# The RWKV recurrence gives each copying engine PSUM tiles of its own

## The chip, the cores and the metric

The kernel runs on one core of a Trainium2 chip. The time is that of one execution on the device, in microseconds: the median over the timed runs. A profiled execution also gives a trace with the start and length of every instruction on the core's engines: TensorE (PE, and PEld for its weight loads), VectorE (DVE), ScalarE (ACT), GpSimd (POOL) and SyncE (SP, which here issues most DMAs). The trace also gives the TensorE clock that was granted, where 1.00 is 2.4 GHz and 0.50 is 1.2 GHz.

## The reference

The reference runs a two-layer block (a sparse-attention mixer and an RWKV-7 mixer, each with a squared-ReLU MLP) and then a second block (two SwiGLU layers around a convolution and mLSTM mixer) over 512 tokens of width 1024. The change touches only the recurrence of the RWKV mixer, which for 16 heads of 64 channels keeps a 64x64 state and updates it token by token:

```
def step(state, inp):
    r_t, w_t, k_t, v_t, kk_t, b_t = inp
    sa = jnp.einsum('bhvk,bhk->bhv', state, -kk_t)
    state = (state * w_t[:, :, None, :] + sa[..., None] * b_t[:, :, None, :]
             + v_t[..., None] * k_t[:, :, None, :])
    y = jnp.einsum('bhvk,bhk->bhv', state, r_t)
    return state, y
```

The outputs y are then normalised per head, scaled, given a bonus term, multiplied by a gate and sent through an output matrix.

## The kernel before

The whole model is one program. Its instructions stand on each engine in the order in which the code writes them; each engine works off its own queue in that order, and semaphores hold an instruction until what it needs is done. The framework gives tiles out of pools in rotation: a new tile of a pool takes the buffer of an old one, and its first writer waits until the old one's readers are done.

The 512 tokens of the recurrence are cut into eight chunks of 64 (0 to 7). Within a chunk the token-by-token recurrence is written as matrix products, for 8 head pairs m and the two heads g of a pair; a head's half of the 128 partitions is LO (g = 0) or HI (g = 1). The function `recurrence` does for chunk c, in this order:

- R: right sides, `kl` times `sv` (L1920), 8 matmuls of K = 128 for m = 0 to 3 and 8 for m = 4 to 7, into one PSUM tile. ScalarE copies each half to `Rs` (L1922).
- TT: a triangular inverse times `Rs` (L1927), in two halves as well, into one PSUM tile. Of each half ScalarE copies the LO partitions and VectorE the HI partitions to `uv` (L1929, L1930).
- KR: `kr` times `sv`, 16 matmuls for the next state (L1935) and 16 for the outputs (L1938).
- BN: `bn` times `uv`, added to the next state (L1942); ScalarE copies its LO half and VectorE its HI half to `SV[c + 1]` (L1943, L1944). The next chunk's R needs both.
- MT: `mt` times `uv`, added to the outputs (L1949); ScalarE copies both halves to `Yn` (L1951).

Between these parts `beside(1)` puts work that does not depend on the state. A local group is one step of `local(c + 1)`: 8 matmuls of `KR` and `BK` (L1781) into a tile of two banks (`pG`, index g chooses the bank), a ScalarE copy to BN (L1782), and VectorE's mask products to MT (L1783) and KL (two, L1787). There are four local groups a chunk, and the last two quarters of the next chunk's KL come from the third and fourth. The other work is a step of `outputs`: for every second chunk it squares the outputs and takes their statistics (L1820 to L1826, `Yn` of two chunks at once; they run in chunks 2, 4 and 6), and later transposes them, multiplies by the gate and splits them into high and low parts (L1796 to L1808); its last part stands right after chunks 3 and 5, ahead of the next R. In chunk 7 there are no local groups, and output-matrix products (`part`) take the place of BN.

The PSUM tiles of R, TT, KR with BN, KR with MT, and the transposes come from pool `psC` (4 banks, one tile each). The local groups have `psG` (2 tiles of two banks).

For each chunk SyncE loads KL, SV and UV (two DMAs of 128 KB each), TT (256 KB), KR and BK (512 KB each) from DRAM, in an order that the code sets; a load waits in that queue until its buffer's last readers are done.

Of the kernel before, what the change touches and what calls it, by code (L numbers as in the profile page):

```python
# [178 lines left out]
class Kernel:  # L179
# [1556 lines left out]
    def recurrence(self, d, EC, sources, gate, nxt):  # L1736
# [3 lines left out]
        nc, tc = self.nc, self.tc  # L1740
        ident = self.c("ident")
        LO, HI = slice(0, 64), slice(64, 128)
# [145 lines left out]
        for c in range(8):  # L1888
# [15 lines left out]
            def group():  # L1904
                return psC.tile([128, 8, 64], F32, name="mm")
# [7 lines left out]

                return ((m, g, HALF[g]) for m in ms for g in G)

            parts = [range(4 * h, 4 * h + 4) for h in range(2)]
            p = group()
            for ms in parts:
                for m, g, s in each(ms):
                    nc.tensor.matmul(p[s, m], kl[:, g, m], sv[:, g, m], start=True, stop=True)  # L1920
                at = slice(ms[0], ms[-1] + 1)
                nc.scalar.copy(Rs[:, at], p[:, at])  # L1922
            beside(1)
            p = group()
            for ms in parts:
                for m, g, s in each(ms):
                    nc.tensor.matmul(p[s, m], TT[c][s, m], Rs[s, m], start=True, stop=True)  # L1927
                at = slice(ms[0], ms[-1] + 1)
                nc.scalar.copy(uv[LO, 0, at], p[LO, at])  # L1929
                nc.vector.tensor_copy(uv[HI, 1, at], p[HI, at])  # L1930
            beside(1)
            if c < 7:
                p = group()
                for m, g, s in each():
                    nc.tensor.matmul(p[s, m], kr[s, 2, m], sv[s, g, m], start=m == 0, stop=False)  # L1935
            py = group()
            for m, g, s in each():
                nc.tensor.matmul(py[s, m], kr[s, 1, m], sv[s, g, m], start=m == 0, stop=False)  # L1938
            beside(1)
            if c < 7:  # L1940
                for m, g, s in each():
                    nc.tensor.matmul(p[s, m], bn[:, g, m], uv[:, g, m], start=False, stop=m == 7)  # L1942
                nc.scalar.copy(SV[c + 1][LO, 0], p[LO])  # L1943
                nc.vector.tensor_copy(SV[c + 1][HI, 1], p[HI])  # L1944
            else:
                part(0, 0)
            beside(1)
            for m, g, s in each():
                nc.tensor.matmul(py[s, m], mt[:, g, m], uv[:, g, m], start=False, stop=m == 7)  # L1949
            for g, s in enumerate(HALF):  # L1950
                nc.scalar.copy(yn[:, g], py[s])  # L1951
            if c % 2 == 1:
                for g in outs:
                    step(g, 100)
# [307 lines left out]
```

## Time and profile before

| what | value |
|---|---|
| median of 3 timed runs | 2447.26 us (2445.79 to 2448.89) |
| the profiled execution's own time | 2448.56 us |
| its span, first to last instruction | 2446.8 us |
| PE busy over the span | 2296.2 us (94%), 12820 matmul records |
| DVE, ACT, POOL busy | 1396.6 us (57%), 1012.5 us (41%), 427.1 us (17%) |
| mean granted TensorE clock | 0.968 |

The span is 1.8 us shorter than the profiled execution's time. Busy shares are means over stages with different limits; the recurrence takes from about 935 to 1042 us of the span. In a timeline, rows of one line that follow each other closely are merged (x16 is 16 records; an fp32 matmul leaves two records), and the bracket gives the engine's idle time before the row and what ended it.

### The profile page before, as it was taken

Reading aid. Unit: us, or ns where it says so; the run is one execution under the profiler, and the core shown is the slowest. Engines: PE = TensorE matmul, PEld = TensorE weight load, DVE = VectorE, ACT = ScalarE, POOL = GpSimd, SP = SyncE. Lnnn points to the kernel's source line nnn. Section 1 sums busy time; section 2 is a strip of 40 time slices with the busy share of each in tenths; the row PEclk is TensorE's granted clock in tenths of the full one; section 3 lists DMA queues with packets and bytes.
Section 4 is the critical chain, followed back from the end, with each engine's and each line's share of the span. In section 5 each row is a group of like instructions: output and inputs, shape, how many; then the busy total and the mean of one; then the engine's idle time right before and its main releaser. Section 6 shows DMA issues by size and latency. Waiting matters only on the chain. (4 is left out here: it accounts for less than half of the span.)

```text
span 2446.8 us, 33701 instructions
## 1 busy us (share of the span) xinstructions
PE 2296.2 (94%) x12820; PEld 1886.1 (77%) x12820; DVE 1396.6 (57%) x2525; ACT 1012.5 (41%) x1903; POOL 427.1 (17%) x430
## 2 busy tenths in 40 slices
PE   7979999999988797789999999999989998999997
PEld 5768888888766676678888888888878886888886
DVE  7987544435788854664444456354466765534445
ACT  5567423324565364443323343332345544333232
POOL 4664100000454731220000020000021013000002
PEclk9999999999989898999999999999999999999998
DMA  4420333233324346432223223223223221323222
GB/s 145 113 75 9 104 98 100 90 99 105 104 69 136 120 142 205 139 104 95 95 95 101 91 84 104 96 94 104 86 76 96 85 79 61 104 95 101 98 89 67
DMA packets 98162, 241.80 MB, mean 99 GB/s; under 512 B 18121, under 2 KB 36937, under 8 KB 98001
## 3 DMA queue, kind: packets, MB, share of 16 engines
q1 hardware_dynamic: 95808, 234.46, 30.4%
q0 software_dynamic: 1040, 3.51, 0.4%
q8 instruction: 101, 1.65, 0.3%
q10 hardware_dynamic: 1152, 1.68, 0.2%
q14 instruction: 61, 0.49, 0.1%
HBM read 214.62 MB, written 19.22 MB: 96 GB/s over the span
## 5 line engine op out<-in xcount | busy, mean ns | idle before, releaser
L147 DVE TENSOR_TENSOR wlo<-wraw,whi 128x512 fp32r<-128x512 f32 (+2 forms) x702 | 513.1, 751 | 447.5 <-ACT whi L146 446.9
L358 PE MATMUL mm<-xh,whi 128*128 128x512 f32 (+3 forms) x1720 | 692.9, 403 | 19.8 <-ACT whi L146 8.2
L359 PE MATMUL mm<-xl,whi 128*128 128x512 f32 (+3 forms) x1720 | 684.1, 398 | 10.0 <-DVE xl L268 8.8
L360 PE MATMUL mm<-xh,wlo 128*128 128x512 f32 (+3 forms) x1720 | 682.8, 397 | 8.7 <-DVE wlo L147 8.6
L146 ACT CAST whi<-wraw 128x512 fp32r<-128x512 f32 (+2 forms) x721 | 430.0, 612 | 522.7 <-PE mm L359 474.4
L358 PEld LDWEIGHTS mm<-xh,whi 128*128 128x128 f32 (+3 forms) x1720 | 329.8, 192 | 96.9 <-issue 12.7
L360 PEld LDWEIGHTS mm<-xh,wlo 128*128 128x128 f32 (+3 forms) x1720 | 329.2, 191 | 83.9 <-DVE wlo L147 12.2
L359 PEld LDWEIGHTS mm<-xl,whi 128*128 128x128 f32 (+3 forms) x1720 | 329.9, 192 | 82.5 <-DVE xl L268 13.2
L358 PE MATMUL mm<-uh,whi 128*128 128x512 f32 (+1 forms) x900 | 346.7, 385 | 0.0
L360 PE MATMUL mm<-uh,wlo 128*128 128x512 f32 (+1 forms) x900 | 344.7, 383 | 0.0
L359 PE MATMUL mm<-ul,whi 128*128 128x512 f32 (+1 forms) x900 | 341.6, 380 | 0.0
L284 POOL TENSOR_TENSOR acc<-acc,sq 128x512 f32<-128x512 f32 (+1 forms) x55 | 73.2, 1331 | 1446.7 <-ACT sq L283 1446.3
L360 PEld LDWEIGHTS mm<-uh,wlo 128*128 128x128 f32 x900 | 168.9, 188 | 36.4
L359 PEld LDWEIGHTS mm<-ul,whi 128*128 128x128 f32 x900 | 169.0, 188 | 34.9
L358 PEld LDWEIGHTS mm<-uh,whi 128*128 128x128 f32 x900 | 169.2, 188 | 31.1
L423 ACT ACTIVATE u<-t 128x512 f32<-128x512 f32 x64 | 40.5, 632 | 192.7 <-DVE t L422 192.7
L422 DVE SCALAR_TENSOR_TENSOR t<-mm,rs 128x512 f32<-128x512 f32 x64 | 44.2, 691 | 89.6 <-PE mm L360 89.3
L436 DVE TENSOR_TENSOR x<-mm,x 128x512 f32<-128x512 f32 x64 | 44.2, 691 | 87.3 <-PE mm L360 87.3
L425 DVE TENSOR_TENSOR ul<-u,uh 128x512 fp32r<-128x512 f32 x64 | 44.3, 692 | 81.1 <-ACT uh L424 81.1
L267 ACT ACTIVATE xh<-x,vec 128x512 fp32r<-128x512 f32 (+1 forms) x50 | 35.2, 705 | 86.0 <-DVE x L436 22.0
L584 ACT CAST uh<-a 128x512 fp32r<-128x512 f32 x44 | 27.3, 621 | 76.4 <-DVE a L583 76.4
L268 DVE SCALAR_TENSOR_TENSOR xl<-x,vec,xh 128x512 fp32r<-128x512 f32 (+1 forms) x50 | 45.2, 908 | 23.5 <-ACT xh L267 23.3
(513 smaller groups left out, 2920.7 us busy)
## 6 DMA issues: line engine op xcount, KB each, us to landing
wraw<-in_ffn_in SPq DMA_DIRECT2D x88, 512.0 KB, 3.7
wraw<-in_up SPq DMA_DIRECT2D x64, 512.0 KB, 3.7
wraw<-in_down SPq DMA_DIRECT2D x64, 512.0 KB, 3.7
wraw<-in_rwkv SPq DMA_DIRECT2D x34, 512.0 KB, 4.8
wraw<-in_ffn_out SPq DMA_DIRECT2D x32, 512.0 KB, 3.7
wraw<-in_mix SPq DMA_DIRECT2D x32, 512.0 KB, 3.7
wraw<-in_dsa SPq DMA_DIRECT2D x23, 512.0 KB, 4.3
wraw<-in_ffn_out SPq DMA_DIRECT2D x16, 384.0 KB, 3.1
```

The source lines that it names most:

```text
L146: self.nc.scalar.copy(hi[:, :per], t)
L147: self.low.tensor_sub(lo[:, :per], t, hi[:, :per].bitcast(F32))
L267: nc.scalar.activation(hi, x, AF.Copy, scale=gm)
L268: nc.vector.scalar_tensor_tensor(lo, x, gm, hi.bitcast(F32), op0=OP.mult, op1=OP.subtract)
L284: (low or (nc.vector if m == NB - 1 else nc.gpsimd)).tensor_add(acc, acc, q[:, s])
L358: nc.tensor.matmul(ps, w[0], x[0], start=start, stop=False)
L359: nc.tensor.matmul(ps, w[0], x[1], start=False, stop=False)
L360: nc.tensor.matmul(ps, w[1], x[0], start=False, stop=stop)
L422: nc.vector.scalar_tensor_tensor(t, p, 0.0, self.rs, op0=OP.max, op1=OP.mult)
L423: nc.scalar.activation(u, t, AF.Square)
L425: nc.vector.tensor_sub(lo, u, hi.bitcast(F32))
L436: nc.vector.tensor_add(self.x[m], p, self.x[m])
```

## The change

The right sides of m = 0 to 3 and of m = 4 to 7 now lie in two PSUM tiles; ScalarE copies the first to `Rs`, VectorE the second. TT runs in one go for all m, with the LO results in one tile and the HI results in another; each engine copies its 64 partitions in one instruction. The next state's sums lie in two tiles in the same way. The KR matmuls for the next state stand right behind TT, ahead of the second local group; those for the outputs stand behind the third local group, after BN. A chunk takes seven tiles from `psC` instead of four.

```diff
--- before.py
+++ after.py
@@ -1913,42 +1913,39 @@
 
                 return ((m, g, HALF[g]) for m in ms for g in G)
 
-            parts = [range(4 * h, 4 * h + 4) for h in range(2)]
-            p = group()
-            for ms in parts:
-                for m, g, s in each(ms):
+
+            for h, copy in enumerate((nc.scalar.copy, nc.vector.tensor_copy)):
+                p, at = group(), slice(4 * h, 4 * h + 4)
+                for m, g, s in each(range(4 * h, 4 * h + 4)):
                     nc.tensor.matmul(p[s, m], kl[:, g, m], sv[:, g, m], start=True, stop=True)
-                at = slice(ms[0], ms[-1] + 1)
-                nc.scalar.copy(Rs[:, at], p[:, at])
+                copy(Rs[:, at], p[:, at])
             beside(1)
-            p = group()
-            for ms in parts:
-                for m, g, s in each(ms):
-                    nc.tensor.matmul(p[s, m], TT[c][s, m], Rs[s, m], start=True, stop=True)
-                at = slice(ms[0], ms[-1] + 1)
-                nc.scalar.copy(uv[LO, 0, at], p[LO, at])
-                nc.vector.tensor_copy(uv[HI, 1, at], p[HI, at])
-            beside(1)
+            ps2 = [group() for _ in G]
+            for m, g, s in each():
+                nc.tensor.matmul(ps2[g][s, m], TT[c][s, m], Rs[s, m], start=True, stop=True)
+            nc.scalar.copy(uv[LO, 0], ps2[0][LO])
+            nc.vector.tensor_copy(uv[HI, 1], ps2[1][HI])
             if c < 7:
-                p = group()
+                ps2 = [group() for _ in G]
                 for m, g, s in each():
-                    nc.tensor.matmul(p[s, m], kr[s, 2, m], sv[s, g, m], start=m == 0, stop=False)
-            py = group()
-            for m, g, s in each():
-                nc.tensor.matmul(py[s, m], kr[s, 1, m], sv[s, g, m], start=m == 0, stop=False)
+                    nc.tensor.matmul(ps2[g][s, m], kr[s, 2, m], sv[s, g, m], start=m == 0, stop=False)
             beside(1)
             if c < 7:
                 for m, g, s in each():
-                    nc.tensor.matmul(p[s, m], bn[:, g, m], uv[:, g, m], start=False, stop=m == 7)
-                nc.scalar.copy(SV[c + 1][LO, 0], p[LO])
-                nc.vector.tensor_copy(SV[c + 1][HI, 1], p[HI])
+                    nc.tensor.matmul(ps2[g][s, m], bn[:, g, m], uv[:, g, m], start=False, stop=m == 7)
+                nc.scalar.copy(SV[c + 1][LO, 0], ps2[0][LO])
+                nc.vector.tensor_copy(SV[c + 1][HI, 1], ps2[1][HI])
             else:
                 part(0, 0)
             beside(1)
+            p = group()
             for m, g, s in each():
-                nc.tensor.matmul(py[s, m], mt[:, g, m], uv[:, g, m], start=False, stop=m == 7)
+                nc.tensor.matmul(p[s, m], kr[s, 1, m], sv[s, g, m], start=m == 0, stop=False)
+            beside(1)
+            for m, g, s in each():
+                nc.tensor.matmul(p[s, m], mt[:, g, m], uv[:, g, m], start=False, stop=m == 7)
             for g, s in enumerate(HALF):
-                nc.scalar.copy(yn[:, g], py[s])
+                nc.scalar.copy(yn[:, g], p[s])
             if c % 2 == 1:
                 for g in outs:
                     step(g, 100)
```

In VectorE's queue, chunk 1 before: masks of the first local group, the two UV copies, masks of the second and third, the SV copy, masks of the fourth. In brackets stand the engines (and DMA queues) whose signals an instruction waits for.

```order
L1783 TENSOR_TENSOR MT<-pG,con 128x2x128 [waits DVE_49,Activation_49]
L1787 TENSOR_TENSOR KL<-pG,con 64x128 [waits DMAHW1_49,DMAHW0_49,DVE_49]
L1787 TENSOR_TENSOR KL<-pG,con 64x128
L1930 COPY UV<-mm 64x256 [waits Activation_49] x2
L1783 TENSOR_TENSOR MT<-pG,con 128x2x128 [waits Activation_49]
L1787 TENSOR_TENSOR KL<-pG,con 64x128 x2
L1783 TENSOR_TENSOR MT<-pG,con 128x2x128 [waits Activation_49]
L1787 TENSOR_TENSOR KL<-pG,con 64x128 x2
L1944 COPY SV<-mm 64x512 [waits DMAHW3_49,DMAHW2_49,Activation_49]
L1783 TENSOR_TENSOR MT<-pG,con 128x2x128 [waits Activation_49]
```

After, in the same chunk, from its new Rs copy on:

```order
L1921 COPY Rs<-mm 128x256 [waits DVE_49,PE_49]
L1783 TENSOR_TENSOR MT<-pG,con 128x2x128 [waits Activation_49]
L1787 TENSOR_TENSOR KL<-pG,con 64x128 [waits DMAHW1_49,DMAHW0_49]
L1787 TENSOR_TENSOR KL<-pG,con 64x128
L1927 COPY UV<-mm 64x512 [waits PE_49]
L1783 TENSOR_TENSOR MT<-pG,con 128x2x128 [waits Activation_49]
L1787 TENSOR_TENSOR KL<-pG,con 64x128 x2
L1937 COPY SV<-mm 64x512 [waits DMAHW2_49,DMAHW3_49,PE_49,Pool_49]
L1783 TENSOR_TENSOR MT<-pG,con 128x2x128 [waits Activation_49]
```

VectorE has one Rs copy more and one UV copy fewer, its SV copy stands ahead of the third group's masks, and its copies of UV and SV wait for PE where they waited for Activation (ScalarE).

On TensorE, chunk 1, the difference (- before, + after; the eight matmuls of each local group, L1781, are left out but for the first and last of a place):

```order
 L1781 MATMUL pG<-KR_7434,BK_7435 64x192
-L1927 MATMUL mm<-Rs,TT_8214 64x64 x16
+L1925 MATMUL mm<-Rs,TT_8214 64x64 x16
+L1931 MATMUL mm<-SV,KR_7433 64x64 x16
...
-L1935 MATMUL mm<-SV,KR_7433 64x64 x16
-L1938 MATMUL mm<-SV,KR_7433 64x64 x16
+L1935 MATMUL mm<-UV,BN 64x64 x16
...
-L1942 MATMUL mm<-UV,BN 64x64 x16
+L1943 MATMUL mm<-SV,KR_7433 64x64 x16
...
-L1949 MATMUL mm<-UV,MT 64x64 x16
+L1946 MATMUL mm<-UV,MT 64x64 x16
```

The state's KR matmuls moved from behind the second local group to ahead of it, next to TT; the outputs' KR matmuls moved from ahead of the third local group to behind it, past BN.

In VectorE's queue, chunk 2, behind the statistics of the norm (the last of them is L1191), before:

```order
L1191 SCALAR_TENSOR_TENSOR y_8792<-t_8793,y_8792 128x16 [waits DVE_49]
L1783 TENSOR_TENSOR MT<-pG,con 128x2x128 [waits Activation_49]
L1787 TENSOR_TENSOR KL<-pG,con 64x128 x2
L1826 TENSOR_TENSOR z<-Yn,y_8792 128x2x8x64 [waits DVE_49]
L1944 COPY SV<-mm 64x512 [waits DMAHW5_49,DMAHW4_49,Activation_49]
L1783 TENSOR_TENSOR MT<-pG,con 128x2x128 [waits Activation_49]
L1787 TENSOR_TENSOR KL<-pG,con 64x128 x2
```

After, up to the next chunk's Rs copy:

```order
L1191 SCALAR_TENSOR_TENSOR y_8812<-t_8813,y_8812 128x16 [waits DVE_49]
L1937 COPY SV<-mm 64x512 [waits DMAHW5_49,DMAHW4_49,PE_49]
L1783 TENSOR_TENSOR MT<-pG,con 128x2x128 [waits Activation_49]
L1787 TENSOR_TENSOR KL<-pG,con 64x128 x2
L1826 TENSOR_TENSOR z<-Yn,y_8812 128x2x8x64 [waits DVE_49]
L1783 TENSOR_TENSOR MT<-pG,con 128x2x128 [waits Activation_49]
L1787 TENSOR_TENSOR KL<-pG,con 64x128 x2
L1921 COPY Rs<-mm 128x256 [waits PE_49]
```

The SV copy moved ahead of the third group's masks and of the product z (L1826); the masks of the third and fourth group stay behind the statistics, and the next chunk's Rs copy follows them.

## Rows read from the trace of the kernel before

**Rows 1.** The stage's window: busy us (instructions) per engine, PEclk, DMA share, GB/s.

```profile
935.46:1041.77 106.31, 80.04 (x1966) 70.89 (x1966) 59.13 (x171) 43.26 (x111) 19.23 (x11) 0.92 0.53 163
```

**Rows 2.** Waits in the stage: who waited for whom, us in total, times, longest.

```profile
PE mm L1927 <- DVE UV L1930: 13.0, 8, 1.8
...
PE mm L1920 <- ACT Rs L1922: 9.3, 8, 1.9
...
PE mm L1920 <- DVE SV L1944: 3.1, 3, 1.5
```

**Rows 3.** Timeline of PE, chunk 1: start, us, instruction, idle before and its releaser.

```profile
950.07 0.64 PE L1920 MATMUL mm<-SV,KL 128*64 128x64 f32 x16
951.91 0.69 PE L1920 MATMUL mm<-SV,KL 128*64 128x64 f32 x16 [1.20 <-ACT Rs L1922]
...
955.41 0.62 PE L1927 MATMUL mm<-Rs,TT 64*64 64x64 f32 x13 [1.76 <-DVE UV L1930]
...
956.37 1.09 PE L1935 MATMUL mm<-SV,KR 64*64 64x64 f32 x31
957.29 1.03 PE L1938 MATMUL mm<-SV,KR 64*64 64x64 f32 x29
...
958.92 1.15 PE L1942 MATMUL mm<-UV,BN 128*64 128x64 f32 x32
960.00 0.88 PE L1781 MATMUL pG<-KR,BK 64*64 64x128 f32 x16
960.81 1.15 PE L1949 MATMUL mm<-UV,MT 128*64 128x64 f32 x32
961.79 0.64 PE L1920 MATMUL mm<-SV,KL 128*64 128x64 f32 x16
```

**Rows 4.** The same view, VectorE and ScalarE, chunk 1: masks, UV, SV.

```profile
954.30 0.59 DVE L1787 TENSOR_TENSOR KL<-pG,con 64x128 f32<-64x128 f32 x2
954.92 0.43 DVE L1930 COPY UV<-mm 64x256 f32<-64x256 f32 x1
...
960.16 0.58 ACT L1943 COPY SV<-mm 64x512 f32<-64x512 f32 x1 [0.74 <-PE mm L1942]
960.77 0.69 DVE L1944 COPY SV<-mm 64x512 f32<-64x512 f32 x1 [0.29 <-ACT SV L1943]
```

**Rows 5.** The same view: square and reduce of chunk 2, last masks.

```profile
968.73 1.06 ACT L1820 ACTIVATE z<-Yn 128x1024 f32<-128x1024 f32 x1
...
969.82 1.22 DVE L1822 TENSOR_REDUCE v<-z 128x16 f32<-128x1024 f32 x1
...
975.67 0.61 DVE L1787 TENSOR_TENSOR KL<-pG,con 64x128 f32<-64x128 f32 x2
```

**Rows 6.** The same view: start of chunk 4, last low parts (xl).

```profile
989.19 0.69 PE L1920 MATMUL mm<-SV,KL 128*64 128x64 f32 x16
...
990.74 0.88 DVE L1808 TENSOR_TENSOR xl<-ot,xh 128x128 fp32r<-128x128 f32 x4
```

**Rows 7.** The same view: chunk 0 and the issue of BK.

```profile
936.70 1.89 DVE L147 TENSOR_TENSOR wlo<-wraw,whi 128x512 fp32r<-128x512 f32 x3 [1.44 <-ACT whi L146]
...
938.03 0.69 PE L1920 MATMUL mm<-SV,KL 128*64 128x64 f32 x16 [1.89 <-ACT Rs L1922]
...
942.78 0.32 SPq L1206 DMA_DIRECT2D BK<-BKD  x1
```

**Rows 8.** DMA issues from 937 to 943 us: tile, KB, median us to landing.

```profile
BK<-BKD SPq DMA_DIRECT2D x1, 512.0 KB, 8.2
```

**Rows 9.** All six BK transfers of the stage.

```profile
DMA to landing us min/median/max: 5.5/5.9/8.2
```

**Rows 10.** Windows in which the clock fell, columns as in rows 1.

```profile
940.00:946.00 6.00, 4.44 (x84) 4.35 (x84) 2.86 (x8) 1.18 (x4) 0.57 (x1) 0.50 1.04 269
980.00:984.00 4.00, 4.00 (x84) 4.00 (x86) 1.43 (x4) 0.74 (x2) 0.86 (x2) 0.57 0.72 212
1032.00:1038.00 6.00, 5.07 (x68) 4.77 (x65) 1.45 (x5) 0.99 (x4) 1.81 (x1) 0.50 0.51 163
```

## Prediction

> **What bounds the kernel now.** I read the table of busy times first, then the stage that the diff touches, then its waits, then one turn of its loop. Over the whole span TensorE is the busiest engine by far; in the recurrence, from the first right-side matmul (935.46 us) to the end of the last output matmul (1041.77), it is busy 80.04 of 106.31 us [rows 1]. So this stage of eight chunks holds 26.3 us in which TensorE idles, and nothing else of the program moves: the order on SyncE and GpSimd stays as it is, and what follows the stage starts from its last output copies and shifts with them.
>
> The waits name the idle time [rows 2]: 13.0 us (8 times) are TT matmuls (L1927) behind VectorE's UV copy, 9.3 us (8 times) the second half of the right sides (L1920) behind ScalarE's Rs copy, 3.1 us (3 times) the first half behind VectorE's SV copy: 25.4 together. A chunk shows how [rows 3]. The first half's matmuls fill a PSUM tile, the second half wants the same tile and has to wait 1.20 us until ScalarE has copied the first, which it does only after two Yn copies; the second half of TT waits 1.76 us until VectorE has copied the first half of UV. VectorE comes late for two reasons [rows 4]: the mask products of a local group (L1783, L1787) stand ahead of it until 954.89, and out of a tile that both copy it starts only when ScalarE is done, as SV shows: ScalarE from 960.16 for 0.58, VectorE at 960.77.
>
> A second loss is the clock: 6.00 us at 0.50 (1.2 GHz) with 4.44 us busy in chunk 0, 4.00 us at 0.57 fully busy in chunk 3, 6.00 us at 0.50 with 5.07 busy in chunk 7 [rows 10]. Busy time times what the clock lacks is 2.2 + 1.7 + 2.5 = 6.4 us. Work at full clock is thus 80.04 − 6.4 = 73.6 us.
>
> **The change part by part.** *Ordinary chunk.* Chunk 1 lasts 961.79 − 950.07 = 11.72 us, without its two waits 8.76 [rows 3]. The prices in it: KR 957.29 − 956.37 = 0.92; a TT half, which is half as many matmuls of that shape, 0.46; a TT half with a local group 956.37 − 955.41 = 0.96, so the group 0.5; a group after KR 958.92 − 957.29 − 0.92 = 0.71; one after BN 0.81.
>
> The right sides now fill two tiles, so the 1.20 us wait goes: R (1.23 us), a local group (0.5), then TT at 1.73. ScalarE's half of Rs is ready 951.91 − 950.07 = 1.84 us after R's start, as the old second half shows. VectorE's half costs what its UV copy of as many elements a partition costs, 0.43 [rows 4], right behind R's end: ready at 1.85. So TT waits 0.1. The two half copies of UV become one of 64x512 on each engine, 0.58 and 0.69 as SV has them. VectorE's masks ended 954.89 − 952.60 = 2.3 us after R's end (951.91 + 0.69); its UV copy would end at 3.0. TensorE meanwhile does group and TT, 0.96 + 0.46, KR 0.92 and a group 0.71: 3.0 us. So BN finds UV just ready, with nothing to spare. This is the cover that shrank, as the 16 output KR matmuls (L1938) moved from ahead of BN to behind it: whatever VectorE is later, BN waits. SV's copies run side by side under a group, KR, a group and MT, over 3 us. I put 0.1 us in each of seven chunks: 0.7.
>
> *Chunk 0.* TT's first half waits for ScalarE until 938.03 [rows 7], where TensorE now is ready at 937.2: 0.8. Its second half waits for VectorE's Rs copy, queued behind three wlo products until 936.70 + 1.89 = 938.59, plus 0.43: until 939.07 instead of 938.49, 0.6.
>
> *Chunk 1, a new wait.* Chunk 0 ends at 935.46 + 8.76 + 1.4 = 945.6, and its successor's first local group would start at 946.9. It needs BK, issued at 942.78 and 8.2 us under way: 951.0 [rows 7, 8]. The issue hangs on SyncE's earlier queue, which this change leaves in its order, so I leave the time. Wait: 4.1 us. The six BK transfers took 5.5 to 8.2 us [rows 9]; with 5.5 the wait is 1.4. I take 8.2, since it is this transfer's own row.
>
> *Chunks 3, 5, 7.* In chunks 2, 4, 6 VectorE works off the norm statistics. From the reduce at 969.82 to the end of the last mask at 975.67 + 0.61 it needs 6.46 us [rows 5]; the same instructions stand there after, only the SV copy is moved ahead. The reduce can start when the second local group is copied by ScalarE (some 0.5 with its start) and the square is done (1.06): 1.84 + 0.92 + 0.92 + 0.71 + 0.5 + 1.06 = 6.0 us into the chunk; the last mask ends at 12.5. The next chunk's last quarter of R needs it and would start at 8.86 + 0.92 = 9.8. So each of the three odd chunks waits 2.7 us: 8.1. Before, chunks like these waited for SV and Rs.
>
> *Chunks 4 and 6.* At their start VectorE still has the transposed outputs: its last low part ends at 990.74 + 0.88 = 991.62, 2.43 us after R's start at 989.19 [rows 6]. The Rs copy stands behind it and ends at 2.9; TT's second half could start at 2.3: 0.6 each, 1.2.
>
> *Chunk 7* has no local group under its Rs copies: 0.15 us.
>
> New waits: 0.7 + 1.4 + 4.1 + 8.1 + 1.2 + 0.15 = 15.7 us instead of 26.3. At full clock the stage lasts 73.6 + 15.7 = 89.3, a gain of 17.0 us. For the clock I keep two falls: one in chunk 1, where TensorE now stands 4.1 us, longer than in any wait of the old stage (price 2.2, as in chunk 0), and one in the three odd chunks (1.7, as in chunk 3): 3.9 us. Gain 13.1 us. The profiled execution took 2448.56 us (span 2446.8); that makes 2435.5. It stands 1.3 us above the median of the three timed runs, 2447.26, so for a median I predict **2434 us**; the rivals' times are counted from that median too.
>
> Unknown costs. TensorE's TT and KR matmuls write two banks in turn, which they did not before. Local groups did (their g picks the bank): 16 records of 128 and 192 columns in 0.81 us, 0.32 ns a column; KR has 32 of 64 in 0.92, 0.45 ns. If two banks bring KR and TT to the groups' pace, 0.27 us goes in each, 15 times: 4.0 us of gain. If two banks cost what a group is dearer after BN than after KR (0.1), 1.5 us of loss. I take 0, since the groups with their two banks are the cheapest per column. The chip's two copying engines reading at once: 0, as ScalarE and VectorE already copy out of different tiles side by side and their copies keep one duration.
>
> **Rivals.** *The clock holds, or the banks help*: no fall gives the full 17.0 us, 2430; the banks' 4.0 us on top of the forecast 17.1, the same. For it: chunk 1 waited 2.96 us in two stretches, and the stage has no falls but those of rows 10. Against: a standstill of 4.1 us. What a page makes of the banks: the Trainium skill, "TensorEngine Tiling (Array Packing)", section "Restrictions and Gotchas", says that different row tiles cannot access one PSUM bank at the same time; by that TT and KR were held back and the gain is real. Rows 3 leave it open.
>
> *The clock falls after every long wait*: chunks 1, 3, 5, 7, at 2.2 and three times 2.5, 9.7 us: gain 7.3, 2440.
>
> *The clock swings in every chunk*, as seven tiles a chunk rotate through the four banks instead of four: 2.2 in seven chunks, 15.4 us: gain 1.6, 2445.7. Against: the pauses between matmul groups get fewer, and the old stage had three falls in eight chunks. A page has this too: the Trainium skill, "TensorE: Matmul & The Clock Gate", section "A second HAM failure mode: psum-queue depth-cycling", tells of a kernel that cycles through PSUM banks, idles briefly between groups and keeps losing its clock; the trace of before bears it out only in the three falls of rows 10.
>
> *Transfers set the chunk (slower).* A chunk loads 2.1 MB (KL, SV, UV and TT 0.26 each, KR and BK 0.52 each). At the 163 GB/s of the whole stage [rows 1] that is 12.9 us, about the mean chunk of 13.3; closer together the transfers could slow each other, as BK's 8.2 us hints. Below 240 GB/s (2.1 MB in 8.76 us) a chunk waits; at 150 GB/s it lasts 14.0, eight of them 5.6 us longer than before: 2453. Against: in chunk 0 the queues moved 269 GB/s [rows 10].
>
> *It doesn't do what it says*: VectorE still waits for ScalarE's copy. The order shows it waiting for TensorE alone. If it did, UV would end 0.6 us later and BN wait as much in seven chunks, 4 us: 2438.
>
> **How the numbers follow.** Forecast 0.54, clock holds or banks help 0.20, falls after every long wait 0.14, doesn't do what it says 0.02, swing in every chunk 0.04, transfers 0.06, of which half ends slower. A measurement of this kernel tells 0.2%, 4.9 us, from no change. The first four are faster by more: 0.90. Same: 0.04 of the swing and 0.03 of the transfers, 0.07; slower 0.03. The range 2428 to 2441 reaches from a little beyond the clock that holds to a little beyond the falls after every wait; outside are swing and transfers, 0.10, and some 0.07 at the edges (both gains of the first rival at once, falls and a late UV at once).
>
> **What would show it.** Right: no wait of TT for UV and of R for Rs; ordinary chunks of about 8.9 us; a wait of the local group in chunk 1 until about 951; R in chunks 3, 5, 7 waiting 2 to 3 us for VectorE's masks; the stage 89 to 93 us long, and the rest of the program as long as before. Wrong: BN waiting for VectorE's UV copy, chunks held by KR or BK after chunk 1, or TT and KR at other durations.

## The result and the profile after

The changed kernel takes 2433.56 us (median of 6 runs), the kernel before 2446.94 (6 runs). The ratio is 0.9943, with a 95% interval of 0.9929 to 0.9956: 0.6% faster, 13.4 us between the medians. The forecast was 2434. In one of the six, the one that was profiled, TensorE was granted 0.69 of its clock from end to end and the kernel took 3068.12 us; the median counts it, the ratio does not (the five others took 2429.96 to 2436.87 us, median 2431.57), and the profile read here is that of a later run of the same kernel, 2435.01 us with a span of 2433.2, which is also the first experiment below.

The windows of the recurrence, first the whole stage, then chunk 1, chunk 2 and the places where the clock fell, and last the 25 us behind the stage (columns as in [rows 1]):

```profile
934.06:1027.78 93.72, 80.63 (x1966) 70.26 (x1966) 60.73 (x171) 38.89 (x95) 19.20 (x11) 0.93 0.61 183
944.79:959.86 15.07, 10.40 (x263) 9.66 (x261) 5.25 (x14) 4.18 (x9) 1.04 (x1) 0.77 0.73 205
959.86:968.68 8.82, 8.82 (x262) 7.73 (x259) 6.05 (x17) 5.03 (x11) 0.00 (x0) 1.00 0.85 285
950.00:955.00 5.00, 4.38 (x84) 4.41 (x88) 1.70 (x4) 0.95 (x2) 0.00 (x0) 0.50 0.88 270
971.80:975.80 4.00, 3.78 (x64) 3.55 (x66) 1.67 (x6) 0.40 (x2) 3.92 (x2) 0.57 0.92 286
1019.00:1023.40 4.40, 4.40 (x50) 4.16 (x50) 1.12 (x2) 0.58 (x1) 3.88 (x2) 0.61 0.01 4
1027.78:1052.78 25.00, 19.49 (x131) 18.26 (x132) 16.24 (x42) 8.93 (x24) 7.00 (x10) 0.86 0.32 105
```

The stage has shrunk from 106.31 us [rows 1] to 93.72, by 12.6; TensorE idles 13.1 us in it, half of the 26.3 of before. Chunk 2 has no idle time at all and lasts 8.82 us, chunk 1 takes 15.07. The profiled execution as a whole is 13.6 us shorter than that of before (2448.56). The stage begins 1.4 us earlier in it, though nothing ahead of the stage was changed: in the profiles whose kernels are the same up to there (before, e1 to e4, e6, e7) it begins between 933.7 and 936.2 us, so a difference of that size between two profiles is no effect of a change.

TensorE's waits in the stage, to be held against [rows 2]:

```profile
PE pG L1781 <- DMA BK<-BKD: 4.7, 1, 4.7
PE mm L1920 <- DVE KL L1787: 4.3, 5, 1.3
PE mm L1925 <- ACT Rs L1921: 1.3, 3, 0.6
PE pG L1781 <- issue: 0.9, 1, 0.9
PE mm L1946 <- issue: 0.7, 1, 0.7
PE mm L1920 <- DVE SV L1937: 0.6, 2, 0.4
PE mm L1943 <- issue: 0.4, 1, 0.4
PE mm L1925 <- DVE Rs L1921: 0.3, 1, 0.3
```

All three waits of before are gone or small: TT waits no more for UV (13.0 us), the right sides no more for Rs (9.3; TT now waits 1.6 for Rs) and 0.6 us instead of 3.1 for SV. In their place stand the wait for BK in chunk 1, the right sides' wait for VectorE's masks (KL), and pauses named "issue", in which TensorE waits for nothing that the profile shows.

The timeline of TensorE: the local group of chunk 1 behind its wait, chunk 2 (as chunk 1 of before in [rows 3]), the right sides of chunk 3, and the last eight of chunks 5 and 7:

```profile
950.62 1.24 PE L1781 MATMUL pG<-KR,BK 64*64 64x128 f32 x14 [4.67 <-DMA BK<-BKD]
...
959.86 1.10 PE L1920 MATMUL mm<-SV,KL 128*64 128x64 f32 x32
960.89 0.88 PE L1781 MATMUL pG<-KR,BK 64*64 64x128 f32 x16
961.70 1.15 PE L1925 MATMUL mm<-Rs,TT 64*64 64x64 f32 x32
962.68 1.03 PE L1931 MATMUL mm<-SV,KR 64*64 64x64 f32 x29
...
964.31 1.15 PE L1935 MATMUL mm<-UV,BN 128*64 128x64 f32 x32
...
968.68 0.28 PE L1920 MATMUL mm<-SV,KL 128*64 128x64 f32 x2
...
972.02 1.00 PE L1920 MATMUL mm<-SV,KL 128*64 128x64 f32 x8 [1.33 <-DVE KL L1787]
972.96 1.24 PE L1781 MATMUL pG<-KR,BK 64*64 64x128 f32 x14
...
995.64 0.76 PE L1920 MATMUL mm<-SV,KL 128*64 128x64 f32 x8 [1.33 <-DVE KL L1787]
...
1018.70 0.76 PE L1920 MATMUL mm<-SV,KL 128*64 128x64 f32 x8 [1.33 <-DVE KL L1787]
```

VectorE in the same two chunks: its Rs and UV copies, the reduce of the statistics, the SV copy, and the last masks, which the right sides at 972.02 waited for (the rows of before are in [rows 4, 5]):

```profile
961.01 0.42 DVE L1921 COPY Rs<-mm 128x256 f32<-128x256 f32 x1 [0.55 <-PE mm L1920]
...
963.30 0.69 DVE L1927 COPY UV<-mm 64x512 f32<-64x512 f32 x1
...
965.79 1.22 DVE L1822 TENSOR_REDUCE v<-z 128x16 f32<-128x1024 f32 x1
...
968.42 0.69 DVE L1937 COPY SV<-mm 64x512 f32<-64x512 f32 x1
...
971.67 0.61 DVE L1787 TENSOR_TENSOR KL<-pG,con 64x128 f32<-64x128 f32 x2
```

UV is copied at 963.99 and BN starts at 964.31: 0.3 us to spare. The last masks end at 972.28, 12.42 us after chunk 2's first matmul.

### The profile page after: what moved, and what is told of

The parts are those of the page before. It is cut to its first block, busy times and chain, and to the rows that moved or that the text cites. A ratio compares the mean times of both kernels' runs of the same rounds, so it can differ in the third digit from the quotient of the medians.

```text
span 3066.3 us, 33705 instructions
## 1 busy us (share of the span) xinstructions
PE 2998.2 (98%) x12820; PEld 2072.9 (68%) x12820; DVE 1403.4 (46%) x2525; ACT 1016.4 (33%) x1887; POOL 421.8 (14%) x430
## 4 chain that ended last, share of the span: by engine, by line
PE 55%; DVE 2%; ACT 0%; POOL 0%; issue 0%; DVEq 0%; ACTq 0%; POOLq 0%
PE mm L359 18%; PE mm L358 18%; PE mm L360 18%; PE pS L1016 1%; PE pN L1063 1%; DVE x L484 1%; DVE h L480 0%; PE pS L1041 0%; DVE xl L268 0%; DVE wlo L147 0%; POOL acc L284 0%; PE st L322 0%; POOL h L480 0%; PE st L463 0%; ACT whi L146 0%
## 5 line engine op out<-in xcount | busy, mean ns | idle before, releaser
L358 PE MATMUL mm<-xh,whi 128*128 128x512 f32 (+3 forms) x1720 | 843.6, 490 | 16.0 <-ACT whi L146 6.4
L359 PE MATMUL mm<-xl,whi 128*128 128x512 f32 (+3 forms) x1720 | 838.4, 487 | 6.7 <-DVE xl L268 6.7
L360 PE MATMUL mm<-xh,wlo 128*128 128x512 f32 (+3 forms) x1720 | 834.4, 485 | 0.2 <-DVE wlo L147 0.2
L358 PEld LDWEIGHTS mm<-xh,whi 128*128 128x128 f32 (+3 forms) x1720 | 353.2, 205 | 195.1 <-issue 46.3
L359 PEld LDWEIGHTS mm<-xl,whi 128*128 128x128 f32 (+3 forms) x1720 | 353.3, 205 | 179.6 <-issue 36.0
L360 PEld LDWEIGHTS mm<-xh,wlo 128*128 128x128 f32 (+3 forms) x1720 | 353.3, 205 | 174.7 <-issue 36.3
L360 PE MATMUL mm<-uh,wlo 128*128 128x512 f32 (+1 forms) x900 | 427.1, 475 | 0.0
L358 PE MATMUL mm<-uh,whi 128*128 128x512 f32 (+1 forms) x900 | 426.6, 474 | 0.0
L359 PE MATMUL mm<-ul,whi 128*128 128x512 f32 (+1 forms) x900 | 425.8, 473 | 0.0
L582 DVE TENSOR_TENSOR b<-mm,rs 128x512 f32<-128x512 f32 x44 | 30.4, 691 | 71.2 <-PE mm L360 71.2
```

The lines of the kernel that those rows point to most:

```text
L358: nc.tensor.matmul(ps, w[0], x[0], start=start, stop=False)
L359: nc.tensor.matmul(ps, w[0], x[1], start=False, stop=False)
L360: nc.tensor.matmul(ps, w[1], x[0], start=False, stop=stop)
```

## The experiments

Times are medians; ratios are to the kernel before, run on the same chip, and come with a 95% interval. They are estimated from all runs and are not the quotients of the medians. The runs were made on three chips (e1 to e4, e5 to e8, e9 to e11; the kernel before took 2448.22, 2447.34 and 2449.27 us there), so versions of different groups are compared by their ratios. Each version has one profile, of one execution.

**e1: the changed kernel again.** No edit.

> The changed kernel once more, with a profile at a clock like that of the kernel before. Theory W (the waits): the recurrence lasts 89 to 93 us instead of 106.3, no wait of TT for UV and none of the right sides for an Rs copy longer than some 0.1 us but in chunk 0; the local group of chunk 1 waits some 4 us for BK; the right sides of chunks 3, 5 and 7 wait 2 to 3 us each for VectorE; about 2434 us, 0.994 of before. Rival B (banks): TT and KR matmuls take 0.6 to 0.7 us in place of 0.92, and the stage is shorter than 89 us although these waits stand. Rival C (clock): the stage's busy time at full clock is shorter by over 2 us, because fewer falls of the clock are left than the three of before, and that, not the waits, makes over a third of the gain.

Measured: 2435.03 us (5 runs, 2434.54 to 2438.74), before 2448.22; ratio 0.9948 (0.9935 to 0.9960). Theory W holds in its parts: the stage at 93.7 us just above its 89 to 93, BK 4.7, chunks 3, 5 and 7 held by VectorE. Rival B falls: KR takes 963.61 − 962.68 = 0.93 us (the next group starts at 963.61), as before (0.92), and TT 962.68 − 961.70 = 0.98, neither of them 0.6 to 0.7. Rival C falls too: the clock costs 5.6 us, against 7.3 before (busy time times what the clock lacks, over the whole of each fall), which is 1.7 of the stage's 12.6 us.

**e2: only UV and the next state in tiles of their own**, the order of before:

```diff
-            p = group()
-            for ms in parts:
...
+            ps2 = [group() for _ in G]
+            for m, g, s in each():
+                nc.tensor.matmul(ps2[g][s, m], TT[c][s, m], Rs[s, m], start=True, stop=True)
+            nc.scalar.copy(uv[LO, 0], ps2[0][LO])
+            nc.vector.tensor_copy(uv[HI, 1], ps2[1][HI])
...
```

> The kernel before, with UV and the next state in two PSUM tiles each, one for an engine (TT in one go); right sides and the place of the KR matmuls as before. Theory W: the 13.0 us of TT behind UV and the 3.1 us of R behind SV go, the 9.3 us of R behind ScalarE's Rs copy stay; in chunks 3, 5 and 7 a wait for VectorE's masks of 1 to 2 us comes in; gain 9 to 12 us, 2435 to 2438 us. Rival S (one chain): the waits are links of one chain, and what UV gives comes back in the wait for Rs; gain under 6 us, above 2441.

Measured: 2435.52 us (5 runs, 2435.01 to 2439.70), ratio 0.9949 (0.9937 to 0.9962). Two rows of its waits in the stage:

```profile
PE mm L1920 <- ACT Rs L1922: 9.1, 8, 1.9
PE mm L1920 <- DVE SV L1942: 3.1, 3, 1.9
```

The time is at the lower end of Theory W's forecast. The wait for UV is gone and that for Rs has not grown (9.3 before): the waits are not links that hand on what they gain, and Rival S falls. This part alone gives as much as the whole change. The wait for SV, which I had expected to go, stayed, and no wait for the masks came in; both stand in the queue of the same VectorE, which is late with the statistics.

**e3: only the right sides in two tiles**, copied by ScalarE and VectorE:

```diff
-            p = group()
-            for ms in parts:
...
+            for h, copy in enumerate((nc.scalar.copy, nc.vector.tensor_copy)):
+                p, at = group(), slice(4 * h, 4 * h + 4)
...
+                copy(Rs[:, at], p[:, at])
```

> The kernel before, with the right sides alone in two PSUM tiles, copied by ScalarE and by VectorE. Theory W: R's 1.2 us waits go (9.3 us), TT's wait for UV grows from 1.76 to some 2.0 us, since the new Rs copy stands ahead of the masks in VectorE's queue; chunks 3, 5 and 7 wait some 2 us for masks where 3.1 us were lost before; gain 4 to 7 us, 2440 to 2443 us. Rival S: TT waits for UV as much longer as R waits less; gain under 2 us, above 2445.

Measured: 2441.43 us (10 runs, 2436.25 to 2445.18), ratio 0.9968 (0.9959 to 0.9978). The 9.3 us of R behind Rs are gone; TT's wait for UV did not grow but is 11.8 us. The time is in Theory W's range; its longer wait for UV did not come.

**e4: the whole change but for the place of KR.** Both groups of KR matmuls stand between the second and the third local group:

```diff
+            beside(1)
             if c < 7:
                 ps2 = [group() for _ in G]
                 for m, g, s in each():
                     nc.tensor.matmul(ps2[g][s, m], kr[s, 2, m], sv[s, g, m], start=m == 0, stop=False)
+            py = group()
+            for m, g, s in each():
+                nc.tensor.matmul(py[s, m], kr[s, 1, m], sv[s, g, m], start=m == 0, stop=False)
             beside(1)
...
```

> The changed kernel with the KR matmuls where they stood before: both for the state and for the outputs between the second and the third local group, BN behind the third. Theory W: BN has more cover for UV, the next right sides have less for SV (a local group and MT, 1.8 us, against copies of 0.6 and 0.7), which is still enough; within 2 us of the changed kernel, 2432 to 2436 us. Rival K (the move counts): R waits for SV by 0.5 us or more in each of seven chunks; 2438 us or more.

Measured: 2430.48 us (5 runs, 2428.41 to 2432.93), ratio 0.9924 (0.9910 to 0.9938): 4.5 us less than the changed kernel on the same chip, and its slowest run is below the fastest of e1. The size is less sure than the sign: the two intervals meet, and three executions of the changed kernel in the result (2429.96 to 2431.57 us) lie in e4's range. Theory W missed this, and Rival K had the wrong sign: the move of KR costs time. Without it the two parts give 17.7 us under the median of before; e2 and e3 gave 12.7 and 6.8. The window of its stage:

```profile
936.24:1023.13 86.89, 76.13 (x1966) 67.20 (x1966) 60.71 (x171) 39.35 (x95) 19.25 (x11) 0.96 0.67 198
```

The five longest of TensorE's waits in it:

```profile
PE pG L1781 <- DMA BK<-BKD: 4.0, 1, 4.0
PE mm L1919 <- DVE SV L1940: 1.7, 2, 1.5
PE pG L1781 <- issue: 1.6, 1, 1.6
PE mm L1924 <- ACT Rs L1920: 1.3, 3, 0.6
PE mm L1945 <- issue: 1.1, 1, 1.1
```

VectorE around its reduce of chunk 2 and its last masks:

```profile
966.48 1.20 DVE L1822 TENSOR_REDUCE v<-z 128x16 f32<-128x1024 f32 x1
...
972.32 0.61 DVE L1787 TENSOR_TENSOR KL<-pG,con 64x128 f32<-64x128 f32 x2
```

Its chunk 2 starts at 961.36, so the reduce starts 5.1 us into the chunk and the masks end at 11.6; in the changed kernel that is 5.9 and 12.4. The state's KR stands ahead of the second local group there, so this group, its masks and the statistics behind them come 0.9 us later, and with them the right sides of the next chunk. The clock falls that the changed kernel has in chunks 3 and 7 (1.7 us each) are missing here. Of the 6.8 us by which the two stages differ, 2.9 are the clock, 2.3 idle time and 1.7 busy time at full clock. I formed Theory T (the later statistics cost the time) from this and split the move.

**e5: chunk 1's loads first.** The changed kernel, with KL, SV, UV and TT of chunk 1 fetched right behind chunk 0's:

```diff
         fetch(0)
+        fetch(1)
...
-                fetch(c + 1)
+                if c:
+                    fetch(c + 1)
```

> The changed kernel, with chunk 1's loads of KL, SV, UV and TT issued right behind chunk 0's, ahead of the weight loads on SyncE that hold its queue until about 936 us, so that BK of chunk 2 is issued some 4 us earlier (at about 937.5 in place of 941.6). Theory W (the wait for BK costs 4.7 us and makes the clock fall, 2.2 us): with 6 to 9 us under way BK lands by 944 to 946.5, the wait and the fall go; 5 to 7 us less than the changed kernel, 2428 to 2430. Rival D (transfers): TensorE then waits for the next transfer of the crowded queues instead, or the earlier loads hold up the weights; within 2 us of the changed kernel or slower.

Measured: 2431.51 us (6 runs, 2429.57 to 2440.59), ratio 0.9938 (0.9918 to 0.9958). Theory W missed its 2428 to 2430, and by the ratios e5 and e1 (0.9948) are not told apart. BK is issued at 938.5 in place of 941.6, and takes almost that much longer. The row of BK of chunk 2 among the DMA issues of e1 (KB, median us to landing):

```profile
BK<-BKD SPq DMA_DIRECT2D x1, 512.0 KB, 8.9
```

The same row in e5:

```profile
BK<-BKD SPq DMA_DIRECT2D x1, 512.0 KB, 11.8
```

The local group starts at 950.37 in place of 950.62. Counted from the stage's start (934.57 and 934.06), BK is issued 3.6 us earlier and lands 0.8 us earlier. The wait for it is 3.3 us for 4.7; the other 0.6 us went into chunk 0, whose pause of issue is 1.3 us for 0.7. From 936 to 943.5 us the DMA engines are 94% busy, at some 290 GB/s; the edit moved 1 MB of loads out of that stretch, and pushed lnw (0.5 MB) and a weight block (0.5 MB) into it.

**e6 and e7: half of the move undone.** In e6 the state's KR stands behind the second local group again, in e7 the outputs' KR ahead of the third:

```diff
+            beside(1)
             if c < 7:
                 ps2 = [group() for _ in G]
                 for m, g, s in each():
                     nc.tensor.matmul(ps2[g][s, m], kr[s, 2, m], sv[s, g, m], start=m == 0, stop=False)
-            beside(1)
```

```diff
             beside(1)
+            py = group()
+            for m, g, s in each():
+                nc.tensor.matmul(py[s, m], kr[s, 1, m], sv[s, g, m], start=m == 0, stop=False)
+            beside(1)
             if c < 7:
...
```

> The changed kernel with the next state's KR matmuls behind the second local group again; those for the outputs stay behind the third. Theory T (start of the statistics): the second local group and with it the norm statistics start 0.9 us earlier in the chunk, so VectorE ends the masks 0.9 us earlier and chunks 3, 5 and 7 wait 1 us less each; with the shorter waits one or both falls of the clock there (1.6 and 1.7 us) go: 3 to 6 us less than the changed kernel, 2429 to 2432. Rival U (it was the outputs' KR that mattered): within 1 us of the changed kernel, 2434 to 2436.

> The changed kernel with the outputs' KR matmuls ahead of the third local group and BN behind it again; the state's KR stay right behind TT. Theory T: the statistics start as late as in the changed kernel and VectorE has the same work ahead of its last masks; within 1 us of the changed kernel, 2434 to 2436. Rival U (the place of the outputs' KR, and of VectorE's SV copy ahead of the third masks, costs the time): 3 to 5 us less, 2430 to 2432.

Measured: e6 2432.17 us (6 runs, 2426.71 to 2438.06), ratio 0.9932 (0.9914 to 0.9950); e7 2432.71 (6 runs, 2430.10 to 2435.70), ratio 0.9933 (0.9918 to 0.9949). Both ratios lie between the changed kernel's and e4's, and both intervals overlap with both: how the 4.5 us divide is not settled. e6 is at the upper edge of Theory T's forecast. For e7 Theory T had foreseen no gain over the changed kernel, Rival U 3 to 5 us, and the ratio is as low as e6's, so Theory T is not shown as the cause of the lost time. In the traces the start of the statistics does what Theory T says: chunk 2's last masks end 11.6 us into the chunk in e6 and 12.4 in e7, as in e4 and in the changed kernel. But e7's right sides wait for SV instead (5.0 us in all), and its clock falls in chunks 1 and 7 alone. The profile of e6, its slowest execution, shows the right sides' wait for the masks halved (2.0 us for 4.3), as many falls of the clock as e1, and pauses of issue of 8.0 us, four times those of e1.

**e8: combined.** e4 with e5's edit, and the product z one step later:

```diff
             r = self.rsqrt(v, 16)
             yield
+            yield
             nc.vector.tensor_mul(z.rearrange("p m h d -> p h m d"), y, r.rearrange("p (h m) -> p h m", h=2)[:, :, :, None]
...
-            for _ in range(4):
+            for _ in range(3):
                 yield
```

> Own tiles for both engines, KR matmuls where they stood in the kernel before, chunk 1's loads issued early, and the product z of the norm one step later, behind the masks of the fourth local group. Theory W and T together: against the version without the move (2430.5) the BK wait of 4.0 us and its clock fall (2.2) go, and the waits of chunks 3, 5 and 7 for VectorE (2 us each, partly under pauses of issue) shrink by the 1.2 us of z: 7 to 10 us less, 2420 to 2424 us. Rival D: the recurrence is then held by transfers or z comes too late for the transposes of the odd chunks (GpSimd has 2.9 us to spare there); above 2427.

Measured: 2433.14 us (6 runs, 2426.68 to 2434.33), ratio 0.9932 (0.9915 to 0.9949): a miss of some 10 us. VectorE's waits are down to 0.3 us for SV, but the transposes wait 4.5 us for GpSimd (3.0 in chunk 7, where I had counted on 2.9 us to spare, and where the clock falls) and TensorE pauses 4.3 us without a releaser. The early loads do more here than in e5. BK is issued at 937.7 (943.9 in e4) and lands at 948.3 (951.4); counted from the stage's start it is issued 4.7 us earlier and lands 1.6 us earlier. BK's row among the DMA issues, and TensorE's wait for it:

```profile
BK<-BKD SPq DMA_DIRECT2D x1, 512.0 KB, 10.6
...
PE pG L1781 <- DMA BK<-BKD: 0.7, 1, 0.7
```

Of the 3.3 us by which this wait is shorter than e4's, the other 1.7 stand in chunk 0 as a pause of issue that e4 does not have there. But the clock stays at 1.00 in chunks 0 to 6, and chunks 0 and 1 together last 22.4 us for 25.1.

**e9: half the loads.** e4 without the loads of KR from chunk 3 on and of BK from chunk 2 on:

```diff
-            nc.sync.dma_start(KR[:, 0:2], d["KR"][c])
-            nc.sync.dma_start(BK, d["BK"][c])
+            if c < 3:
+                nc.sync.dma_start(KR[:, 0:2], d["KR"][c])
+            if c < 2:
+                nc.sync.dma_start(BK, d["BK"][c])
```

> The version without the move of KR, which loads KR only for chunks 0 to 2 and BK only for chunks 0 and 1; later chunks compute with these (1.0 of 2.1 MB a chunk is left out). It tells what the pauses of TensorE are that wait for nothing in the profile (issue; 2.8 us there). Theory I (TensorE's instructions arrive late because the loads crowd the DMA engines): the pauses shrink to under 0.5 us in the recurrence, the BK wait (4.0) and its clock fall (2.5) go; 8 to 9 us less, 2421 to 2423 us. Rival J (the instruction stream itself is too slow for matmuls of 64 columns): the pauses stay at 2 to 5 us; 2424 to 2427 us.

Measured: 2424.28 us (5 runs, 2420.14 to 2429.41), ratio 0.9908 (0.9893 to 0.9924). All waits of TensorE in its stage:

```profile
PE mm L1921 <- DVE SV L1942: 4.2, 3, 1.5
PE pG L1783 <- DMA KR<-KRD: 2.8, 1, 2.8
PE mm L1926 <- ACT Rs L1922: 1.5, 3, 0.6
PE mm L1798 <- POOL z L1832: 0.6, 1, 0.6
PE mm L1926 <- DVE Rs L1922: 0.3, 1, 0.3
```

No pause of issue is left in this profile, where e4 had 2.7 us, as Theory I has it. The time does not fit it: 2424.28 lies above its 2421 to 2423 and in Rival J's range. In the trace KR took the place of BK as the late load of chunk 1, the clock fell there all the same (0.87), and the wait for SV, which the pauses had covered in e4, shows in full: 4.2 us for 1.7.

That TensorE waits for its instructions in these pauses can be read from the traces. The profile has a DMA queue of the kind "instruction" (q8), which moves packets of 16 KB on the same 16 engines as the loads. All 39 pauses named issue in the stages of the twelve profiles (before and e1 to e11) end 1.2 to 1.7 us after such a packet ends; TensorE's other waits end 0.0 to 8.5 us after one. In the 4 us ahead of these 39 packets the DMA engines were 0.68 to 1.02 busy, as they were ahead of 74 other packets; none of the 67 packets behind a less busy stretch was followed by a pause. One of the 39, in e1, starts at 941.66 and takes 1.25 us (the queue's packets, MB and share of 16 engines' time from 941 to 942), and the pause ends at 944.33:

```profile
q8 instruction: 1, 0.02, 7.8%
...
944.33 0.62 PE L1946 MATMUL mm<-UV,MT 128*64 128x64 f32 x14 [0.68 <-issue]
```

**e10: the same loads of chunk 1 at another place**, behind lnw and ahead of the two weight blocks that hold SyncE's queue:

```diff
             gate(m, psC.tile([128, T], F32, name="mm"))
+            if m == 4:
+                fetch(1)
...
-                fetch(c + 1)
+                if c:
+                    fetch(c + 1)
```

> The version without the move of KR, with chunk 1's loads of KL, SV, UV and TT behind lnw and ahead of the two weight loads of SyncE's queue, in the stretch (931 to 938 us) in which the DMA engines were not full. Theory D2 (BK comes late because the loads of 936 to 950 us are more than the DMA engines move at some 300 GB/s, so what counts is bytes moved out of that stretch): 1 MB less stands there, BK lands 3 us earlier, the wait of 4.0 us falls under 1 us and the clock does not fall (2.5); 4 to 6 us less, 2424 to 2427 us. Rival: the weights come in its place, BK lands when it did; within 1.5 us of that version, 2429 to 2432.

Measured: 2427.68 us (5 runs, 2423.84 to 2432.03), ratio 0.9915 (0.9900 to 0.9930). The window of its stage:

```profile
933.75:1017.14 83.39, 74.24 (x1966) 65.04 (x1966) 60.68 (x171) 39.35 (x95) 19.23 (x11) 1.00 0.67 208
```

Two of TensorE's waits in it:

```profile
PE mm L1948 <- issue: 2.5, 3, 1.4
...
PE pG L1781 <- DMA BK<-BKD: 1.2, 1, 1.2
```

BK's wait falls from 4.0 to 1.2 us (Theory D2: under 1) and the clock stays at 1.00 through the whole stage, which is 3.5 us shorter than e4's, as Theory D2 has it in the trace. But counted from the stage's start BK is issued 4.2 us earlier than in e4 and lands 1.5 us earlier (Theory D2: 3), and the rest of the shorter wait is a pause of 1.4 us in chunk 0, much as in e8, whose loads stand at e5's place. So the run does not show that the bytes moved out of the stretch are what counts. The median is just outside the forecast, and by the ratios e10 and e4 are not told apart (0.9915 and 0.9924).

**e11: e10 with z one step later, as in e8, and in halves**, so that GpSimd is done early with the first half:

```diff
...
+            yield
+            rm = r.rearrange("p (h m) -> p h m", h=2)
+            for f in range(2):
+                m = slice(4 * f, 4 * f + 4)
+                nc.vector.tensor_mul(z[:, m].rearrange("p m h d -> p h m d"), y[:, :, m],
+                                     rm[:, :, m, None].to_broadcast([128, 2, 4, 64]))
+                zf = z[:, m].rearrange("p m h d -> p (m h d)")
+                nc.gpsimd.tensor_mul(zf, zf, lnw[:, f * T:(f + 1) * T])
+                nc.gpsimd.tensor_add(zf, zf, bt[:, f * T:(f + 1) * T])
...
```

> As loads between, and the product z of the norm stands behind the masks of the fourth local group, in two halves, each followed by GpSimd's work on that half, so that the first transposes need only the first half. Theory T: the right sides of chunks 3, 5 and 7 no longer wait for VectorE (0.2 and 1.5 us, and 2 us under pauses of issue), the transposes wait under 0.5 us for GpSimd (3.0 in chunk 7 with z in one piece); 2 to 4 us less than loads between, 2421 to 2424 us. Rival I2 (TensorE runs into its own instruction supply): the gain turns into pauses of issue, 4 us or more of them in the recurrence; within 1 us of loads between.

Measured: 2423.07 us (4 runs, 2421.63 to 2428.91), ratio 0.9901 (0.9885 to 0.9917). It beats the kernel before by 1.0% and the changed kernel, whose interval in e1 ends at 0.9935. The time is in Theory T's range. GpSimd's wait is 0.5 us, VectorE's waits 0.7 and 0.8; in return its profile has 5.2 us of pauses of issue and 2.2 of BK, in a stage of 84.94 us, 1.6 longer than in e10's profile. In the traces the gain went into pauses, as Rival I2 says; in the medians e11 is 4.6 us below e10, with runs that overlap.

## Why the prediction was right, step by step

**Own tiles.** Right. TT waits no more for UV and VectorE's copies start without ScalarE's: UV on ScalarE from 962.88 and on VectorE from 963.30. That the change doesn't do what it says is out. e2 and e3 show that each part frees its own wait.

**Ordinary chunk.** Right: 8.86 us foreseen, 8.82 measured in chunk 2. UV was to be ready just when BN can start and came 0.3 us ahead; the 0.7 us that I had put there did not come.

**Banks.** Right at 0. TT and KR write two banks in turn, KR lasts as long as before, and TT takes 0.98 us where two halves of 0.46 were counted. The Trainium skill, "TensorEngine Tiling (Array Packing)", section "Restrictions and Gotchas", has row tiles kept from one PSUM bank at the same time; by that TT and KR should have run faster once each head had a bank of its own. No run here shows that: KR takes 0.92 us before and 0.93 after.

**Chunk 0.** Mis-sized: 1.4 us foreseen, 0.61 + 0.27 = 0.9 measured. (The 939.07 in the working adds up to 939.02.)

**Chunk 1.** The wait was right (4.1 foreseen, 4.7 measured; BK landing at about 951, the group at 950.62) and so was the fall of the clock behind it (2.2 us). The cause was half right: I named the issue on SyncE's queue and let the transfer keep its 8.2 us. Counted from the stage's start, BK is issued 3.6, 4.7 and 4.2 us earlier in e5, e8 and e10 (than in e1, e4 and e4) and lands only 0.8, 1.6 and 1.5 us earlier. Each time it is some 3 us longer under way, with the DMA engines 93 to 97% busy from 936 to 943.5 us. So an earlier issue is paid back for the most part in the transfer; what sets the landing beyond that was not separated. The rival in which transfers set the chunk was thus real, but for chunk 1 only; chunk 2 moves 285 GB/s without a wait.

**Chunks 3, 5, 7.** Right in the main: masks that end 12.5 us into the chunk were foreseen and end at 12.42 in chunk 2. From the first right-side matmul to the next work (the local group; TT in chunk 7), less the 1.03 us that they take undisturbed, it is 3.2, 2.0 and 3.2 us: 8.4 for a forecast of 8.1. The waits view shows 4.9 of it; the rest stands inside rows of right-side matmuls that last longer. Some 0.9 us of it is not the masks': 0.6 is the wait for SV, and in chunk 3 the last eight matmuls take 0.25 us longer than in chunk 5, at the lower clock.

**Chunks 4 and 6.** Mis-sized and with another releaser: 0.3 us each behind ScalarE's Rs copy, not 0.6 behind VectorE's.

**The clock.** Too mild: two falls with 3.9 us foreseen, three with 5.6 measured (chunks 1, 3 and 7: 2.2, 1.7 and 1.7). "Falls after every long wait" was nearly it, with chunk 5 left out; 2440 was too high as the falls of chunks 3 and 7 cost 1.7 and not 2.5. The loss of before was also read too small: the windows of [rows 10] cut off the ends of two falls. From 939.26 to 946.09 us TensorE was busy 5.27 us at 0.50, from 1031.42 to 1038.25 5.90 us; with chunk 3 that is 7.3 us and not 6.4, and the work at full clock 72.7 and not 73.6. The swing in every chunk is out: chunks 0, 2, 4, 5 and 6 run at 1.00 with seven tiles in four banks. The Trainium skill, "TensorE: Matmul & The Clock Gate", section "A second HAM failure mode: psum-queue depth-cycling", would have let one fear it; this trace does not show it.

**What was missing.** The pauses of issue: 0.9 us before, 2.0 after. The forecast's stage was 73.6 us of work at full clock, 15.7 of waits and 3.9 for the clock, 93.2 in all. Measured are 75.0 us of busy time at full clock (with the waits that stand inside rows), 13.1 of idle time and 5.6 for the clock: 93.7. So errors of both signs cancelled, and the stage gained 12.6 us against 13.1. That the total came as close as 2433.56 to 2434 is luck in part: it holds 1.7 us of clock loss more than foreseen, and the other five runs of the result have a median of 2431.57.

The forecast left open what the move of KR does alone. I counted its cover for UV and for SV and found both sufficient; that it also delays the second local group, and all that VectorE has behind it, is contained in the 6.0 us at which I let the reduce start, but I did not see it as a price of the move. e4 shows 4.5 us for the move; that the late statistics are what costs it is argued from its trace and not shown (e6 and e7).

## What to carry to other kernels

When two engines copy out of one PSUM tile, give each a tile of its own and price it per wait; here each part gave back its own wait and nothing was handed on to another of the old waits (new ones, for BK and for the masks, came in). Before moving a block ahead of independent work, ask which queue of another engine that work feeds: here a move that covered everything it was meant to cover made VectorE's statistics and last masks 0.9 us later, and the kernel without it took 4.5 us less. Once TensorE stops waiting, look at what the DMA engines still have to bring in that stretch; a load that is issued earlier into a crowded stretch takes longer, so only part of the head start arrives (0.8 of 3.6 us in e5, 1.6 of 4.7 in e8). When TensorE pauses without a releaser there, look at the instruction queue among the DMA queues.

## What the runs showed of the hardware that was not expected

- TensorE pauses without a releaser where loads fill the DMA engines: 0.9 us in the stage before, 2.0 after, 8.0 in e6's profile, none in e9 with half the loads. All 39 of them end 1.2 to 1.7 us after a 16 KB packet of the instruction queue that came behind 4 us with the DMA engines at least 0.68 busy. Whether they account for the spread of the times (11 us among e6's runs) is not shown, since each version has one profile.
- With the DMA engines 93 to 97% busy, a 512 KB load took 11.8 (e5), 10.6 (e8) and 10.2 us (e10) to land where 5.5 to 8.2 were seen before [rows 9].
- In the 25 us behind the stage, where TensorE waits 2.4 us for VectorE, the granted clock was 0.93 before and 0.86 after, and 0.81 to 1.00 in the other versions, with the same instructions: 0 to 3.7 us for the clock. e2, whose gain in the stage is like the whole change's, has 0.93 as before, so whether the change or the single execution sets it is not shown.
